# A hybrid decoder layer: thirteen of the MLP's 22 column-tile pairs by Strassen's scheme

## The chip, the cores and the metric

The kernel runs on one core of one Trainium2 chip. The metric is the device time of one execution in microseconds (us). The core has five engines with a queue each: TensorE (PE; its weight loads are a row of their own, PEld), VectorE (DVE), ScalarE (ACT), GpSimd (POOL) and SyncE (SP), which here only issues transfers.

## The reference

One decoder layer on 512 tokens of width 1024, all in float32. Three token mixers (a gated short convolution, block-sparse attention, cross-attention to a memory) are gated, merged and projected, and a residual is added. The change touches what follows:

```
h2 = rmsnorm(x, g_ffn)
a, b = jnp.split(h2 @ w_up, 2, axis=-1)        # w_up: 1024 x 5632
a = causal_dwconv3(a, ffn_conv_w, ffn_conv_b)   # three taps over positions, per channel
x = x + (jax.nn.silu(a) * b) @ w_down           # w_down: 2816 x 1024
```

## The kernel before, in words

Activations lie with channels on the 128 partitions and the 512 tokens along the row. A float32 product is made of three matmuls on a rounded format, `mm3`: each operand is split into a high part (rounded, by ScalarE) and a low part (the rest, by VectorE), and high x high, low x high and high x low add up in one PSUM bank (L235 to L237). A block of weights is 128x128; `weight_units` lists the blocks in the order of use, and they lie in that order in memory. They come in pieces of eight blocks (512 KB, three `raw` buffers, `load_piece`, issued by SP at L180). `cut_steps` makes the high part of a piece on ScalarE (`hi`, L197) and the low part on VectorE (`lo`, L200), with three buffers of each.

w_up has 44 column tiles of 128: 22 for `a`, 22 for `b`; tile f of `a` and tile f of `b` make a pair. The first two pairs run side by side (`proj_outer`: for each of eight row blocks k, four banks). Each later pair is two tiles of eight blocks, so 48 matmuls of 512 columns (`proj_inner`). The inputs `h2` are x times the gain, not yet divided by the norm. That factor, `r2b`, one number per token spread over the partitions, is multiplied in when a bank is read (L871, L878). `ffn_a` reads the bank of `a` into `u`, whose first two columns GpSimd clears, runs the three taps (`conv3`: one ScalarE and two VectorE instructions, L582 to L584) and SiLU (L873); `ffn_b` reads the bank of `b`, multiplies (L879) and splits the product for w_down (L242, L244). w_down then takes four column tiles at once, three singly and the last in two halves of 256 tokens.

The order of TensorE's instructions is that of the program. On the other four engines a scheduler sets the order of each queue when the program is built; each engine then runs its queue strictly in that order, each instruction waiting for what it needs.

Of the kernel before, what the change touches and what calls it, by code (L numbers as in the profile page):

```python
# [59 lines left out]
def weight_units():  # L60

    u = []

    def inner(m, c, nk):
        u.extend((m, k, c) for k in range(nk))

    def outer(m, cs, nk):
        u.extend((m, k, c) for k in range(nk) for c in cs)

    outer("w_in", range(T_QM, T_QM + 4), KD)  # L70
    for c in range(4):
        inner("w_mem_kv", c, KD)
    outer("w_mem_kv", range(4, 8), KD)
    for c in range(4):
        for t in (T_C, T_X, T_B):
            inner("w_in", t + c, KD)
    for p in range(4):
        if p == 3:
            outer("w_in", range(T_V, T_V + 4), KD)
        inner("w_in", T_Q + p, KD)  # L80
        inner("w_in", T_K + p, KD)
    for g, m, ahead in ((0, "w_br_conv", 0), (2, "w_br_mem", 0), (1, "w_br_moba", AHEAD)):
        n = max(ahead, 1)
# [27 lines left out]
def layer_kernel(ctx: ExitStack, tc: tile.TileContext, xT, memT, vecs, ws, outT):  # L111
    nc = tc.nc
    units = weight_units()
    sizes = piece_sizes(len(units))

    cp = ctx.enter_context(tc.tile_pool(name="cp", bufs=1))
    wp = ctx.enter_context(tc.tile_pool(name="wp", bufs=3))
    tp = ctx.enter_context(tc.tile_pool(name="tp", bufs=10))
    ps = ctx.enter_context(tc.tile_pool(name="ps", bufs=1, space=bass.MemoryType.PSUM))
    hp = ctx.enter_context(tc.tile_pool(name="hp", bufs=16))  # L120
    mp = ctx.enter_context(tc.tile_pool(name="mp", bufs=8))
# [13 lines left out]
    def bank(tag="acc"):  # L135
        return ps.tile([P, 512], F32, tag=tag, name=nm(tag), bufs=PSB[tag])
# [232 lines left out]
    start = ExitStack()  # L369
# [47 lines left out]
    mh, hx, qm_n, kk, km, vm = ([] for _ in range(6))  # L417
# [65 lines left out]
    first = []  # L483
# [354 lines left out]
    x2, h2 = [], []  # L838
    ss_2 = yp.tile([P, S], F32, tag="yr", name="ss_2", bufs=7)

    def residual(acc, k):
# [3 lines left out]
        split(hl, x, V("g_ffn", k))  # L845
        x2.append(x)
# [12 lines left out]
    mid.close()  # L859


    fp = ctx.enter_context(tc.tile_pool(name="fp", bufs=2 * NF))
    r2b = fp.tile([P, S], F32, tag="r2b", name="r2b", bufs=1)
    mlp = []
    for _ in row_steps(r2b, small(16), ss_2):
        pass

    def ffn_a(acc, f):
        u = tp.tile([P, S + 2], F32, tag="u", name=nm("u"), bufs=2)
        nc.gpsimd.memset(u[:, 0:2], 0.0)  # L870
        nc.vector.tensor_mul(u[:, 2 : S + 2], acc, r2b)  # L871
        t = conv3(u, [V("f_w", NF * i + f) for i in range(3)], V("f_b", f))
        nc.scalar.activation(t, t, AF.Silu)  # L873
        return t

    def ffn_b(acc, t):
        b = tmp()
        nc.vector.tensor_mul(b, acc, r2b)  # L878
        nc.vector.tensor_mul(b, b, t)  # L879
        hl = tuple(fp.tile([P, S], FR, tag="m", name=nm("m")) for _ in range(2))  # L880
        split(hl, b)
# [82 lines left out]
```

## Time and profile before

| | |
|---|---|
| median of 3 runs | 843.8 us (841.82 to 844.9) |
| the profiled execution | 844.19 us |
| its span, first to last instruction | 842.4 us |
| TensorE busy | 834.2 us, 3714 matmuls |
| VectorE / ScalarE / GpSimd busy | 519.9 / 380.8 / 46.2 us |
| w_up, from its first to its last matmul's start | 469.1 to 715.3 us |
| w_down | 715.5 us to the end |
| mean granted TensorE clock | 0.997 of 2.4 GHz |

Matmuls overlap in the trace: one of 512 columns is shown as 0.39 us long, but the next starts before it ends. What a row of them costs is read from the distance between starts. VectorE's instructions overlap a little too, so for them as well the distance between starts is the price in a full queue, and the duration is the time until somebody else can use the result.

### The profile page before, as it was taken

To read this page: it belongs to the slowest core of one execution; us is meant where nothing else is said; L and a number is where in the kernel's file an instruction comes from. 1 tells how busy PE (TensorE), PEld (TensorE's weight loads), DVE (VectorE), ACT (ScalarE), POOL (GpSimd) and SP (SyncE) were. 2 spreads that over 40 slices of the span, in tenths; PEclk is the share of its full clock that TensorE was granted. 3 is DMA by queue.
4 is the path that set the end of the run, shared out by engine and by line. 5 is a ranking of instruction groups with operands and counts; after the bars stand their busy time and mean duration, and the time that the engine had idled before them with its cause. 6 is when DMAs were issued, how large, how long until landed. Compare 5 with 4: busy or idle time off the path is not lost.

```text
span 842.4 us, 9986 instructions
## 1 busy us (share of the span) xinstructions
PE 834.2 (99%) x3714; PEld 679.3 (81%) x3714; DVE 519.9 (62%) x834; ACT 380.8 (45%) x682; POOL 46.2 (5%) x97
## 2 busy tenths in 40 slices
PE   8999999999999999999999999999999999999998
PEld 6788888888888888888888888888888888888888
DVE  5998898957767776755547575565556655323221
ACT  6666776637645655553324453333333333222110
POOL 0200000101221101110000000000000000000000
PEclk9999999999999999999999999999999999999999
DMA  8353222433333332225223223322332232223410
GB/s 298 112 172 101 96 76 80 123 114 105 100 100 113 95 100 75 82 93 177 99 100 100 79 96 100 100 83 92 100 101 85 90 100 100 96 81 128 135 63 26
DMA packets 26594, 87.76 MB, mean 104 GB/s; under 512 B 3121, under 2 KB 3761, under 8 KB 26417
## 3 DMA queue, kind: packets, MB, share of 16 engines
q1 hardware_dynamic: 26400, 87.04, 31.9%
q8 instruction: 29, 0.48, 0.2%
q14 instruction: 21, 0.16, 0.1%
q10 hardware_dynamic: 144, 0.08, 0.0%
HBM read 81.87 MB, written 2.10 MB: 100 GB/s over the span
## 4 chain that ended last, share of the span: by engine, by line
PE 95%; DMA 2%; DVE 2%; issue 0%; ACT 0%; SPq 0%; DVEq 0%; ACTq 0%
PE acc L237 25%; PE acc L236 25%; PE acc L235 25%; PE s L236 6%; PE s L237 6%; PE s L235 6%; PE m L752 1%; DMA raw<-ws 1%; PE s L693 1%; DMA xr<-xT 1%; PE s L694 1%; DVE lo L200 0%; DVE mh L248 0%; DVE ss_x L433 0%; PE m L237 0%
## 5 line engine op out<-in xcount | busy, mean ns | idle before, releaser
L197 ACT ACTIVATE hi<-raw 128x1024 fp32r<-128x1024 f32 (+1 forms) x148 | 154.9, 1047 | 263.8 <-PE acc L237 154.9
L200 DVE TENSOR_TENSOR lo<-raw,hi 128x1024 fp32r<-128x1024 f32 (+1 forms) x148 | 179.4, 1213 | 152.5 <-ACT hi L197 152.2
L237 PE MATMUL acc<-h,hi 128*128 128x512 f32 x568 | 224.3, 395 | 0.0
L235 PE MATMUL acc<-h,hi 128*128 128x512 f32 x568 | 224.3, 395 | 0.0
L236 PE MATMUL acc<-h,lo 128*128 128x512 f32 x568 | 224.2, 395 | 0.0
L237 PEld LDWEIGHTS acc<-h,hi 128*128 128x128 f32 x568 | 106.8, 188 | 25.5
L236 PEld LDWEIGHTS acc<-h,lo 128*128 128x128 f32 x568 | 106.8, 188 | 24.9
L235 PEld LDWEIGHTS acc<-h,hi 128*128 128x128 f32 x568 | 106.8, 188 | 24.7
L236 PE MATMUL acc<-m,lo 128*128 128x512 f32 (+1 forms) x132 | 47.1, 357 | 0.0
L235 PE MATMUL acc<-m,hi 128*128 128x512 f32 (+1 forms) x132 | 47.1, 357 | 0.0
L237 PE MATMUL acc<-m,hi 128*128 128x512 f32 (+1 forms) x132 | 47.1, 357 | 0.0
L235 PE MATMUL s<-h,hi 128*128 128x512 f32 x112 | 44.2, 395 | 0.0
L236 PE MATMUL s<-h,lo 128*128 128x512 f32 x112 | 44.2, 395 | 0.0
L237 PE MATMUL s<-h,hi 128*128 128x512 f32 x112 | 44.2, 395 | 0.0
L300 ACT ACTIVATE ty<-ty 32x16 f32<-32x16 f32 (+4 forms) x136 | 29.1, 214 | 16.4 <-DVE ty L281 8.0
L873 ACT ACTIVATE tmp<-tmp 128x512 f32<-128x512 f32 x22 | 14.0, 636 | 41.2 <-DVE tmp L584 41.1
L871 DVE TENSOR_TENSOR u<-acc,r2b 128x512 f32<-128x512 f32 x15 | 10.4, 692 | 31.7 <-PE acc L237 31.7
L236 PEld LDWEIGHTS acc<-m,lo 128*128 128x128 f32 x132 | 24.8, 188 | 4.1
L235 PEld LDWEIGHTS acc<-m,hi 128*128 128x128 f32 x132 | 24.8, 188 | 4.0
L237 PEld LDWEIGHTS acc<-m,hi 128*128 128x128 f32 x132 | 24.8, 188 | 4.0
L780 ACT ACTIVATE tmp<-acc,half_b 128x512 f32<-128x512 f32 x21 | 14.5, 688 | 29.9 <-PE acc L237 29.8
L235 PE MATMUL s<-m,hi 128*128 128x512 f32 x66 | 26.1, 395 | 0.0
(218 smaller groups left out, 1359.7 us busy)
## 6 DMA issues: line engine op xcount, KB each, us to landing
raw<-ws SPq DMA_DIRECT2D x145, 512.0 KB, 3.3
xr<-xT SPq DMA_DIRECT2D x8, 256.0 KB, 5.7
xres<-xT SPq DMA_DIRECT2D x1, 2048.0 KB, 9.5
outT<-tmp SPq DMA_DIRECT2D x7, 256.0 KB, 3.1
qh<-qh SPq DMA_DIRECT2D x12, 128.0 KB, 2.3
ql<-ql SPq DMA_DIRECT2D x12, 128.0 KB, 2.3
mr<-memT SPq DMA_DIRECT2D x4, 256.0 KB, 7.7
raw<-ws SPq DMA_DIRECT2D x2, 128.0 KB, 3.1
```

Source lines behind the costliest of these rows:

```text
L197: nc.scalar.activation(hi[:, :m], raw[:, :m], AF.Copy)
L200: nc.vector.tensor_sub(lo[:, :m], raw[:, :m], hi[:, :m].bitcast(F32))
L235: nc.tensor.matmul(out, l[0], r[0], start=start, stop=False)
L236: nc.tensor.matmul(out, l[1], r[0], start=False, stop=False)
L237: nc.tensor.matmul(out, l[0], r[1], start=False, stop=stop)
L300: nc.scalar.activation(dst, src, AF.Copy)
L693: nc.tensor.matmul(acc[:, :n], l, q_hi[:, q0:], start=True, stop=False)
L694: nc.tensor.matmul(acc[:, :n], l, q_lo[:, q0:], start=False, stop=True)
L752: nc.tensor.matmul(acc[:, i0:], l, b[:, : S - i0], start=i == 0 and b is x[0], stop=i == 3 and b is x[1],)
L780: nc.scalar.activation(z, acc, AF.Tanh, bias=half_b[:, i : i + 1], scale=0.5)
L871: nc.vector.tensor_mul(u[:, 2 : S + 2], acc, r2b)
L873: nc.scalar.activation(t, t, AF.Silu)
```

## The change

For 13 pairs (FAST: f = 3 to 5, 7 to 9, 11 to 13, 15 to 17 and 19) the product of a pair is done by Strassen's scheme, in the form with 15 additions. The matrix of weights for a pair is cut in four: rows 0 to 511 and 512 to 1023 (four blocks k each), columns of `a` and of `b`. The inputs are cut in four in the same way: channels, and tokens 0 to 255 and 256 to 511. Seven products of a quarter with a quarter take the place of eight. Each is four blocks k of three matmuls with 256 columns (`product`), so a pair has 84 matmuls of 256 columns in place of 48 of 512.

What is added around them:

- The factor `r2b` is now multiplied into x after the first two pairs (`hn`: eight VectorE multiplies and eight splits), and the other pairs read no `r2b`.
- Four sums of the inputs (`sums`, from 16 VectorE subtractions of 256 columns and eight splits) are made once.
- For each fast pair, `cut_fast` makes four sums of the weights: three by VectorE (s3, s2, s4, into `sx`), the fourth, a21 + a22, by a transfer that GpSimd issues and that adds to its destination in place. Then it splits all seven operands.
- For the 18 pieces of w_up that are not in fast pairs the low part is no longer a VectorE subtraction: ScalarE writes the negated high part, and a GpSimd transfer adds the raw weights to it.
- Seven reads of PSUM per fast pair add the products up (`fast_tiles`: two by ScalarE, five by VectorE, 256 columns each), four banks x, y, z, w, of which three take a second product.
- Products for w_down are kept whole (`mf`) and split after the last pair. x itself goes to memory and is read back for the last residual.

```diff
+FAST = frozenset((3, 4, 5, 7, 8, 9, 11, 12, 13, 15, 16, 17, 19))
...
         nc.scalar.activation(hi[:, :m], raw[:, :m], AF.Copy)
         st["cut"] = i + 1
         yield
-        nc.vector.tensor_sub(lo[:, :m], raw[:, :m], hi[:, :m].bitcast(F32))
+        if units[sum(sizes[:i])][0] == "w_up":
+
+            nc.scalar.activation(lo[:, :m], raw[:, :m], AF.Copy, scale=-1.0)
+            nc.gpsimd.dma_start(lo[:, :m], raw[:, :m], accum_op=ALU.add)
+        else:
+            nc.vector.tensor_sub(lo[:, :m], raw[:, :m], hi[:, :m].bitcast(F32))
...
+    hn = []
+    for k in range(KD):
+        nc.vector.scalar_tensor_tensor(
+            x2[k], x2[k], V("g_ffn", k), r2b, op0=ALU.mult, op1=ALU.mult
+        )
+        hl = tuple(hp.tile([P, S], FR, tag="h", name=nm("hn")) for _ in range(2))
+        split(hl, x2[k])
+        hn.append(hl)
+
+    sums = [[] for _ in range(4)]
+    for k in range(0, KH, 2):
+        raw = [tmp() for _ in range(4)]
+        for i in range(2):
+            top, low, c = x2[k + i], x2[k + i + KH], slice(H * i, H * i + H)
+            t1, t2, t3, t4 = (r[:, c] for r in raw)
+            nc.vector.tensor_sub(t1, top[:, H:], top[:, :H])
+            nc.vector.tensor_sub(t2, low[:, H:], t1)
+            nc.vector.tensor_sub(t3, low[:, H:], top[:, H:])
+            nc.vector.tensor_sub(t4, low[:, :H], t2)
+        for n, r in enumerate(raw):
+            hl = tuple(fs.tile([P, S], FR, tag="t", name=nm("t"), bufs=16) for _ in range(2))
+            split(hl, r)
+            sums[n].extend(tuple(a[:, H * i : H * i + H] for a in hl) for i in range(2))
...
+    def cut_fast():
...
+        nc.vector.tensor_sub(s3, a11, a21)
+        nc.vector.tensor_sub(s2, a22, s3)
+        nc.vector.tensor_sub(s4, a12, s2)
+        nc.gpsimd.dma_start(a21, a22, accum_op=ALU.add)
+        f1 = tuple(wp.tile([P, 2 * n], FR, tag=t, name=nm(t), bufs=3) for t in ("hi", "lo"))
+        fx = tuple(fs.tile([P, 3 * n], FR, tag=t, name=nm(t), bufs=2) for t in ("hx", "lx"))
+        f2 = tuple(wp.tile([P, 2 * n], FR, tag=t, name=nm(t), bufs=3) for t in ("hi", "lo"))
+        split(tuple(a[:, :n] for a in f1), a11)
+        split(fx, sx)
+        split(tuple(a[:, n:] for a in f1), a21)
+        split(f2, r2)
...
+    def product(out, l, r, first):
+        for k in range(KH):
+            w = tuple(a[:, k * P : (k + 1) * P] for a in l)
+            for x, (a, b) in enumerate(((w[0], r[k][0]), (w[1], r[k][0]), (w[0], r[k][1]))):
+                nc.tensor.matmul(
+                    out[:, :H], a, b, start=first and k == 0 and x == 0,
+                    stop=k == KH - 1 and x == 2, skip_group_check=not first,
+                )
+
+    def fast_tiles(f, l, tags):
...
+        product(x, a11, rows(0, 0), True)
+        nc.scalar.activation(v1, x[:, :H], AF.Copy)
+        product(y, s2, sums[1], True)
+        nc.vector.tensor_add(v2, y[:, :H], v1)
+        product(z, s3, sums[2], True)
+        nc.vector.tensor_add(v1, z[:, :H], v2)
+        product(w, s1, sums[0], True)
+        nc.vector.tensor_add(b[:, H:], w[:, :H], v1)
+        product(x, a12, rows(KH, 0), False)
+        nc.scalar.activation(u[:, 2 : H + 2], x[:, :H], AF.Copy)
+        product(z, a22, sums[3], False)
+        nc.vector.tensor_add(b[:, :H], z[:, :H], v2)
+        product(w, s4, rows(KH, H), False)
+        nc.vector.tensor_add(u[:, H + 2 :], w[:, :H], v2)
+        gated(conv3(u, *taps(f)), b)
...
     for f in range(2, NF):
-        tag = "s" if f % 3 == 2 else "acc"
-        t = ffn_a(proj_inner("w_up", f, h2, tag=tag), f)
-        ffn_b(proj_inner("w_up", NF + f, h2, tag=tag), t)
...
+        tags = ("acc",) * 4 if f % 2 == 0 else ("s", "m", "s", "m")
+        if f in FAST:
+            fast_tiles(f, left, tags)
```

The scheduler's order changes with it, at three places that the prediction speaks of. On VectorE, where the first two pairs end, the queue before holds the bank reads of pairs 0 and 1, their taps, and the low parts of the next weights (`u`, `tmp`: the two pairs; `lo`: weights; the number in a name tells tiles apart):

```order
L871 TENSOR_TENSOR u_929_4646<-acc_913_4522,r2b_4501 128x512
L878 TENSOR_TENSOR tmp_931_4654<-acc_914_4523,r2b_4501 128x512
L871 TENSOR_TENSOR u_934_4661<-acc_915_4524,r2b_4501 128x512
L583 SCALAR_TENSOR_TENSOR tmp_930_4649<-u_929_4646,vec_77,tmp_930_4649 128x512
L878 TENSOR_TENSOR tmp_936_4669<-acc_916_4525,r2b_4501 128x512
L584 SCALAR_TENSOR_TENSOR tmp_930_4649<-u_929_4646,vec_77,tmp_930_4649 128x512
L200 TENSOR_TENSOR lo_941_4678<-raw_925_4590,hi_940_4677 128x1024
```

Now 42 instructions stand from the read of the first bank (`u_929`) up to `t_972`, the low part of the second half of `sums[1]`. These are the last of them (`t_...`: split sums of the inputs; `lo_1001`, `sx_999`: weights of pair 4; `tmp_978`: taps of pair 2):

```order
L257 TENSOR_TENSOR t_964_4755<-tmp_956_4733,t_963_4754 128x512
L257 TENSOR_TENSOR t_970_4771<-tmp_965_4758,t_969_4770 128x512
L952 TENSOR_TENSOR sx_999_4972<-raw_998_4970,sx_999_4972 128x512
L930 TENSOR_TENSOR tmp_968_4761<-x2_896_4457,tmp_966_4759 128x256
L896 TENSOR_TENSOR mf_936_4687<-tmp_935_4685,tmp_934_4681 128x512
L1006 SCALAR_TENSOR_TENSOR tmp_978_4811<-acc_977_4786,vec_77,tmp_978_4811 128x511
L930 TENSOR_TENSOR tmp_968_4761<-x2_904_4499,tmp_966_4759 128x256
L257 TENSOR_TENSOR lo_1001_4978<-raw_997_4968,hi_1000_4977 128x512
L257 TENSOR_TENSOR t_972_4775<-tmp_966_4759,t_971_4774 128x512
```

So the sums of the inputs stand behind the taps of pairs 0 to 2 and between parts of the weights of pairs 3 and 4. On TensorE the second product of pair 3 (bank `m_989`) takes that tile after its first half:

```order
L972 MATMUL m_989_4863<-t_959_4746,hx_984_4850 128x256
L972 MATMUL m_989_4863<-t_959_4746,lx_985_4851 128x256
L972 MATMUL m_989_4863<-t_960_4747,hx_984_4850 128x256
L972 MATMUL m_989_4863<-t_971_4774,hx_984_4850 128x256
L972 MATMUL m_989_4863<-t_971_4774,lx_985_4851 128x256
L972 MATMUL m_989_4863<-t_972_4775,hx_984_4850 128x256
```

On GpSimd the queue before held only the clearings of `u` here:

```order
L870 MEMSET u_943_4707 128x2
L870 MEMSET u_956_4784 128x2
L870 MEMSET u_969_4861 128x2
L870 MEMSET u_982_4938 128x2
L870 MEMSET u_995_5015 128x2
```

Now the adding transfers stand between them (`raw` into `raw`: the sum a21 + a22 of a fast pair; `raw` into `lo`: a low part of a plain pair; here from the clearing for pair 7 to the first piece of pair 10):

```order
L981 MEMSET u_1056_5324 128x2
L954 DMA raw_1040_5241<-raw_1041_5243 128x512
L211 DMA lo_1038_5236<-raw_1036_5233 128x1024
L981 MEMSET u_1074_5453 128x2
L954 DMA raw_1061_5426<-raw_1062_5428 128x512
L954 DMA raw_1079_5555<-raw_1080_5557 128x512
L981 MEMSET u_1092_5582 128x2
L211 DMA lo_1099_5687<-raw_1097_5684 128x1024
```

There are two `u` buffers, so a clearing waits until the taps two fast pairs earlier have been read, and the transfers behind it wait with it.

## Rows read from the trace of the kernel before

**Rows 1.** The page: busy time of each engine, and the chain that ended last.
```profile
PE 834.2 (99%) x3714; PEld 679.3 (81%) x3714; DVE 519.9 (62%) x834; ACT 380.8 (45%) x682; POOL 46.2 (5%) x97
...
PE 95%; DMA 2%; DVE 2%; issue 0%; ACT 0%; SPq 0%; DVEq 0%; ACTq 0%
```
**Rows 2.** Windows: length, then busy PE, PEld, DVE, ACT, POOL, PEclk, DMA, GB/s.
```profile
469.00:491.50 22.50, 22.50 (x99) 18.08 (x98) 12.07 (x23) 9.29 (x11) 0.00 (x0) 1.00 0.30 94
491.50:603.00 111.50, 111.50 (x479) 89.71 (x478) 68.27 (x87) 44.74 (x55) 1.19 (x12) 1.00 0.29 94
```
**Rows 3.** Timeline of PE: start, us, instruction; where w_up starts and later.
```profile
469.07 0.40 PE L235 MATMUL acc<-h,hi 128*128 128x512 f32 x1
...
491.47 0.40 PE L235 MATMUL s<-h,hi 128*128 128x512 f32 x1
...
494.27 0.40 PE L235 MATMUL s<-h,hi 128*128 128x512 f32 x1
```
**Rows 4.** Timeline of PE and of PEld, last column tile, 256 columns.
```profile
828.02 0.28 PE L236 MATMUL acc<-m,lo 128*128 128x256 f32 x1
...
834.08 0.28 PE L236 MATMUL acc<-m,lo 128*128 128x256 f32 x1
...
823.28 0.19 PEld L236 LDWEIGHTS acc<-m,lo 128*128 128x128 f32 x1
823.40 0.19 PEld L237 LDWEIGHTS acc<-m,hi 128*128 128x128 f32 x1
```
**Rows 5.** Windows early in the run, and PE's timeline inside them.
```profile
33.00:35.00 2.00, 1.51 (x8) 1.00 (x8) 2.00 (x3) 0.00 (x0) 1.84 (x3) 1.00 0.00 0
35.00:37.00 2.00, 0.83 (x5) 0.72 (x4) 2.00 (x2) 1.06 (x1) 0.15 (x1) 0.74 0.00 0
37.00:39.00 2.00, 2.00 (x11) 2.00 (x10) 2.00 (x4) 0.00 (x0) 0.00 (x0) 0.50 0.91 274
...
37.09 0.41 PE L236 MATMUL s<-mh,lo 128*128 128x256 f32 x1
37.30 0.41 PE L237 MATMUL s<-mh,hi 128*128 128x256 f32 x1
```
**Rows 6.** Timeline of DVE: four instructions of a full queue, then r2b.
```profile
449.31 1.22 DVE L200 TENSOR_TENSOR lo<-raw,hi 128x1024 fp32r<-128x1024 f32 x1
450.44 0.69 DVE L853 TENSOR_TENSOR ss<-ss,tmp 128x512 f32<-128x512 f32 x1
451.05 0.75 DVE L248 SCALAR_TENSOR_TENSOR h<-x,vec,h 128x512 fp32r<-128x512 f32 x1
451.71 0.68 DVE L853 TENSOR_TENSOR ss<-ss,tmp 128x512 f32<-128x512 f32 x1
...
479.80 0.71 DVE L288 STREAM_TRANSPOSE r2b<-ty 128x512 f32<-128x512 f32 x1
```
**Rows 7.** Timeline of DVE: the first read of a w_up bank.
```profile
489.58 0.69 DVE L871 TENSOR_TENSOR u<-acc,r2b 128x512 f32<-128x512 f32 x1 [1.18 <-PE acc L237]
```
**Rows 8.** Groups of ACT in w_up: busy, mean ns, idle before.
```profile
L197 ACT ACTIVATE hi<-raw 128x1024 fp32r<-128x1024 f32 x44 | 46.7, 1062 | 100.2 <-PE acc L237 65.4 <-PE s L237 27.9 <-issue 6.8
...
L242 ACT ACTIVATE m<-tmp 128x512 fp32r<-128x512 f32 x21 | 13.3, 633 | 9.0 <-DVE tmp L879 8.9
```
**Rows 9.** The page: transfers, KB each, median us from issue to landing.
```profile
raw<-ws SPq DMA_DIRECT2D x145, 512.0 KB, 3.3
...
xres<-xT SPq DMA_DIRECT2D x1, 2048.0 KB, 9.5
outT<-tmp SPq DMA_DIRECT2D x7, 256.0 KB, 3.1
qh<-qh SPq DMA_DIRECT2D x12, 128.0 KB, 2.3
```
**Rows 10.** POOL: a clearing of u in the timeline, and its longest group.
```profile
493.71 0.10 POOL L870 MEMSET u<- 128x2 f32 x1 [126.44 <-DVE tmp L584]
...
L711 POOL PARTITION_ALL_REDUCE mb<-tmp x8 | 14.7, 1843 | 10.9 <-DVE tmp L709 10.9
```

More of the change, by code (lines that the diff above doesn't have):

```diff
@@ L94, in weight_units @@
     for f in range(2, NF):
-        inner("w_up", f, KD)
-        inner("w_up", NF + f, KD)
+        if f in FAST:
+            for ks in (range(4), range(4, KD)):
+                for c in (f, NF + f):
+                    u.extend(("w_up", k, c) for k in ks)
+        else:
+            inner("w_up", f, KD)
+            inner("w_up", NF + f, KD)
     outer("w_down", range(4), NF)
@@ L839, in layer_kernel @@
     ss_2 = yp.tile([P, S], F32, tag="yr", name="ss_2", bufs=7)
+    dp = ctx.enter_context(tc.tile_pool(name="dp", bufs=1, space=bass.MemoryType.DRAM))
+    x2d = dp.tile([KD, P, S], F32, name="x2d")
     def residual(acc, k):
@@ L845, in residual @@
         split(hl, x, V("g_ffn", k))
+        nc.sync.dma_start(x2d[k], x)
         x2.append(x)
@@ L859, in layer_kernel @@
     mid.close()
-    fp = ctx.enter_context(tc.tile_pool(name="fp", bufs=2 * NF))
-    r2b = fp.tile([P, S], F32, tag="r2b", name="r2b", bufs=1)
-    mlp = []
+    H = S // 2
+    KH = KD // 2
+    fm = ctx.enter_context(tc.tile_pool(name="fm", bufs=NF - 8, reuse_waits="tile"))
+    fast = ExitStack()
+    fs = fast.enter_context(tc.tile_pool(name="fs", bufs=1, reuse_waits="tile"))
+    r2b = fm.tile([P, S], F32, tag="r2b", name="r2b", bufs=1)
+    mf = []
     for _ in row_steps(r2b, small(16), ss_2):
@@ L866, in layer_kernel, with taps, gated @@
         pass
-    def ffn_a(acc, f):
+    def taps(f):
+        return [V("f_w", NF * i + f) for i in range(3)], V("f_b", f)
+    def gated(t, b):
+        pool, tag = (fm, "mf") if len(mf) < NF - 8 else (mp, "mj")
+        m = pool.tile([P, S], F32, tag=tag, name=nm("mf"))
+        nc.scalar.activation(t, t, AF.Silu)
+        nc.vector.tensor_mul(m, b, t)
+        mf.append(m)
+    accs = proj_outer("w_up", (0, NF, 1, NF + 1), h2, ["acc"] * 4)
+    st["look"] = 0
+    for f in range(2):
         u = tp.tile([P, S + 2], F32, tag="u", name=nm("u"), bufs=2)
@@ L870, in ffn_a @@
         nc.gpsimd.memset(u[:, 0:2], 0.0)
[L871 to L876, printed above, removed]
-        b = tmp()
[L878 to L881, printed above, removed]
-        mlp.append(hl)
-    accs = proj_outer("w_up", (0, NF, 1, NF + 1), h2, ["acc"] * 4)
@@ L885, in layer_kernel @@
-    for f in range(2):
-        ffn_b(accs[2 * f + 1], ffn_a(accs[2 * f], f))
-    for f in range(2, NF):
-        tag = "s" if f % 3 == 2 else "acc"
-        t = ffn_a(proj_inner("w_up", f, h2, tag=tag), f)
-        ffn_b(proj_inner("w_up", NF + f, h2, tag=tag), t)
-    def finish(acc, c, cols=slice(0, S)):
-        o = tmp()
-        nc.vector.tensor_add(o[:, cols], acc[:, cols], x2[c][:, cols])
+        nc.vector.tensor_mul(u[:, 2 : S + 2], accs[2 * f], r2b)
+        t = conv3(u, *taps(f))
+        b = tmp()
@@ new lines, in layer_kernel @@
+        nc.vector.tensor_mul(b, accs[2 * f + 1], r2b)
+        gated(t, b)
+    hn = []
[20 more added lines that the diff above has]
+            sums[n].extend(tuple(a[:, H * i : H * i + H] for a in hl) for i in range(2))
@@ new lines, in rows, with part @@
+    def rows(k0, c0):
+        return [tuple(a[:, c0 : c0 + H] for a in hn[k]) for k in range(k0, k0 + KH)]
+    def cut_fast():
+        i = st["cut"]
+        while st["loaded"] < i + 2:
+            load_piece()
+        r1, r2 = raws.pop(i), raws.pop(i + 1)
+        st["cut"] = i + 2
+        n = KH * P
+        a11, a21 = r1[:, :n], r1[:, n:]
+        a12, a22 = r2[:, :n], r2[:, n:]
+        sx = fs.tile([P, 3 * n], F32, tag="sx", name=nm("sx"))
+        s2, s3, s4 = (sx[:, n * j : n * j + n] for j in range(3))
+        nc.vector.tensor_sub(s3, a11, a21)
[9 more added lines that the diff above has]
+        split(f2, r2)
+        def part(hl, j):
+            return tuple(a[:, n * j : n * j + n] for a in hl)
+        return part(f1, 0), part(fx, 0), part(fx, 1), part(f1, 1), part(f2, 0), part(f2, 1), part(fx, 2)
@@ new lines, in product @@
+    def product(out, l, r, first):
[7 more added lines that the diff above has]
+    def fast_tiles(f, l, tags):
+        a11, s2, s3, s1, a12, a22, s4 = l
+        x, y, z, w = (bank(t) for t in tags)
+        u = tp.tile([P, S + 2], F32, tag="u", name=nm("u"), bufs=2)
+        nc.gpsimd.memset(u[:, 0:2], 0.0)
+        b, v = tmp(), tmp()
+        v1, v2 = v[:, :H], v[:, H:]
+        product(x, a11, rows(0, 0), True)
[13 more added lines that the diff above has]
+        gated(conv3(u, *taps(f)), b)
@@ new lines, in plain_tiles, with cut_next @@
+    def plain_tiles(f, tags):
+        acc = proj_inner("w_up", f, hn, tag=tags[0])
+        ws, bias = taps(f)
+        t = tmp()
+        nc.scalar.activation(t, acc, AF.Identity, bias=bias, scale=ws[2])
+        for i in (1, 2):
+            nc.vector.scalar_tensor_tensor(
+                t[:, i:], acc[:, : S - i], ws[2 - i], t[:, i:], op0=ALU.mult, op1=ALU.add
+            )
+        gated(t, proj_inner("w_up", NF + f, hn, tag=tags[1]))
+    def cut_next(f):
+        if f in FAST:
+            return cut_fast()
+        for _ in range(2 if f < NF else 0):
+            while st["cut"] < st["use"] + 2:
+                cut_piece()
@@ new lines, in layer_kernel @@
+    left = None
+    for f in range(2, NF):
+        tags = ("acc",) * 4 if f % 2 == 0 else ("s", "m", "s", "m")
+        if f in FAST:
+            fast_tiles(f, left, tags)
+            st["u"] += 2 * KD
+            st["use"] += 2
+        else:
+            plain_tiles(f, tags)
+        if f == max(FAST):
+            fast.close()
+        left = cut_next(f + 1)
+    st["look"] = LOOK
+    fd = ctx.enter_context(tc.tile_pool(name="fd", bufs=2 * NF - 16, reuse_waits="tile"))
+    mlp = []
+    for f in range(NF):
+        pool, tag = (fd, "m") if f < NF - 8 else (hp, "h")
+        hl = tuple(pool.tile([P, S], FR, tag=tag, name=nm("m")) for _ in range(2))
+        split(hl, mf[f])
+        mlp.append(hl)
@@ L895, in finish, with stream @@
+    def stream(c):
+        x = tmp()
+        nc.sync.dma_start(x, x2d[c])
+        return x
+    def finish(acc, c, o, cols=slice(0, S)):
+        nc.vector.tensor_add(o[:, cols], acc[:, cols], o[:, cols])
         nc.sync.dma_start(outT[c * P : (c + 1) * P, cols], o[:, cols])
+    outs = [stream(c) for c in range(4)]
     for c, acc in enumerate(proj_outer("w_down", range(4), mlp, ["acc"] * 4)):
-        finish(acc, c)
+        finish(acc, c, outs[c])
     for c in range(4, 7):
-        finish(proj_inner("w_down", c, mlp, tag="s"), c)
+        o = stream(c)
+        finish(proj_inner("w_down", c, mlp, tag="s"), c, o)
@@ L902, in layer_kernel @@
     parts = [(bank(), slice(0, S // 2)), (bank(), slice(S // 2, S))]
     head = NF - 8
+    o = stream(7)
     ws = []
@@ L912, in layer_kernel @@
             mm3(acc[:, cols], ws[k], tuple(a[:, cols] for a in mlp[k]), False, k == NF - 1)
-        finish(acc, 7, cols)
+        finish(acc, 7, o, cols)
 def kernel(**inputs):
```

1 line of the change is left out of this document (added).

## The prediction, written before the result was known

> **What bounds the kernel now.** I read the page's busy times and its chain first: TensorE is busy 99% of the span and the chain runs through it for 95% [rows 1]. Then I cut w_up out by windows: in 491.5 to 603 us TensorE is busy 111.5 of 111.5 us at a granted clock of 1.00, VectorE 68.3, ScalarE 44.7 [rows 2]. Last, TensorE's own timeline: twelve matmuls of 512 columns start in 494.27 - 491.47 = 2.80 us, 0.2333 us each, and two pairs (96 matmuls) take 491.47 - 469.07 = 22.40 us, again 0.2333 [rows 3]. So here TensorE waits for nothing. Every matmul's worth that goes is time won, as long as nobody makes TensorE wait; every wait that comes in is time lost, since no gap can swallow it. The sum is therefore: work removed from TensorE, against waits put in.
>
> **What goes.** A pair now is 48 x 0.2333 = 11.20 us. A fast pair is 84 matmuls of 256 columns. Such matmuls stand in the last column tile: 51 steps in 834.08 - 828.02 = 6.06 us, 0.119 us each [rows 4], hence 84 x 0.119 = 10.00 us. 1.20 us per pair, 13 pairs: **15.6 us less**. An eighth of the columns goes, but a short matmul costs 2% more than half a long one.
>
> A rule of the Trainium skill speaks against this term ("TensorE: Matmul & The Clock Gate", Part 3, what overlaps and what doesn't): a weight load overlaps matmuls in flight only when it goes to another group of the array's rows. Rows 4 show loads over all 128 rows, 0.19 us long and 0.12 us apart, beside steps of 0.119 us: the rule does not hold for this kernel.
>
> **What it puts on the other engines.** By steps in a full queue VectorE's instruction costs 1.13 us at 1024 columns, 0.61 at 512, 0.66 for one with a scalar and two tensors [rows 6]; a line through the first two gives 0.35 at 256 and 1.65 at 1536 (estimates). A fast pair asks three weight sums (1.83), the low parts (2 x 0.61 + 1.65 + 1.13 = 4.00), five reads of banks (1.75), two taps (1.32) and a gate product (0.61): 9.5 us in TensorE's 10.0. A plain pair keeps 1.9 us, since its low parts leave VectorE. Averaged over w_up it fits; inside a fast pair nothing may be late. ScalarE's per-pair sum (its 1024-column copy is 1.06 us, its 512-column one 0.63 [rows 8]) stays under 7 us.
>
> **Front, a wait on VectorE (certain to come; its size is the main term).** r2b's write ends at 480.5 [rows 6]; I put it at 481.0, as one more ScalarE copy stands ahead. From then the queue has 8 multiplies by r2b (8 x 0.66 = 5.3) and 9 subtractions (5.5) ahead of the first bank read, which so starts near 491.8 and not at 489.58 [rows 7]; TensorE's pair 2 starts about 1.1 us late. From that read to t_972, 42 instructions: 19 of 512 columns (11.6), 16 of 256 (5.6), 5 taps (3.3), one each of 1024 and 1536 (2.8) = 23.3 us, so t_972 starts at 515.1 and is there at 515.8. TensorE wants it after pair 2 (491.47 + 11.20), pair 3's first product (1.43) and half of the second (0.71), with 0.24 of starts between: 505.05. **10.7 us lost.** Within it, t_971 comes from ScalarE, where it stands behind hi_1000, which waits for an adding transfer; it does not come later than VectorE's own queue allows. Behind the wait nothing is late at once: the scheduler's next weights go on being cut.
>
> **Clock.** TensorE would stand about 5 us and then 3 us with six matmuls between. The trace shows one such place: after a stretch of 8 and then 5 matmuls in 2 us each, the granted clock is 0.74 and then 0.50 (the 1.2 GHz level), and 256-column starts are 0.214 us apart instead of 0.119 [rows 5]. It ran low for 3.4 us there. The same here costs 3.4 x (1 - 0.119/0.214) = **1.5 us**. Bounds 0 and 3.
>
> **Adding transfers.** 18 of 512 KB (low parts of plain pieces) and 13 of 256 KB (a21 + a22) are issued by GpSimd and read what they write. The trace has none. Nearest rows from below: a raw load of 512 KB, 3.3 us, and a copy of 128 KB, 2.3 [rows 9]. From above a second read is added: 2 MB takes 9.5 us and 512 KB 3.3, 4.13 us per MB, so 512 KB more is 2.1 us: 5.4; and 256 KB, 3.1 + 1.0 = 4.1. I take the middle of each, 4.4 and 3.2 us, and 1 us of GpSimd per issue (0.10 for a clearing, 1.84 for its longest instruction [rows 10]). What follows a fast pair's transfer is fixed: raw buffer free, next load (3.3), transfer, ScalarE's copies, VectorE's low part, 9.5 us plus the transfer, against 12.4 us of TensorE's work from that buffer's release to its use in the next pair. So with 3.2 it is 0.3 us over in the second and third pair of a run of three. On GpSimd the transfers stand behind the clearings of u, so one late tap keeps back the weights of a later pair. On ScalarE and VectorE a copy that waits for a transfer holds the next bank's read behind it.
>
> I laid the five queues of w_up end to end in their new order with the durations above. Waits of TensorE from 469 us on, all told (front included):
>
> - transfers 3.3 and 2.3 us: 11.2 us
> - 4.4 and 3.2: 12.6 us (GpSimd at 0.5 or 1.5 us an issue: 11.9, 14.1)
> - 5.0 and 3.6: 18.0 us
> - 5.4 and 3.7: 21.3 us
> - 6.0 and 4.8: 30.4 us
>
> Up to 4.4 only the front counts; beyond it each fast pair pays about 1.3 us twice, as the first read of its last banks waits.
>
> **Costed at nothing.** The added factor and the sums beyond the front, and the reads of r2b that go, are VectorE's, not on the path later. Storing x and reading it back adds SP issues that nobody waits for before the last residual. w_down's first weights are loaded under w_up's last pairs; the 22 late splits (ScalarE 22 x 0.63 = 13.9 us, VectorE about 13.4) run beside pairs 20 and 21 and w_down's first tiles, 14 row blocks of 12 matmuls, 39 us of TensorE's work, before the last ones are wanted. If that cover is gone they cost up to 13 us, less the idle time of VectorE there; I see no place for more than 1.
>
> **Sum**, against the profiled execution of 844.19 us (842.4 of span, 1.8 around it): 844.2 - 15.6 + 12.6 + 1.5 = 842.7. It lies 0.4 above the median of 843.8, so the forecast is **842.3 us**: gain and waits nearly cancel. No change that a measurement of this kernel can tell, within 0.5%, is 839.6 to 848.0.
>
> **Rivals.**
>
> 1. *Slower: the adding transfers set the pace.* Mechanism: in a fast pair VectorE reads two tensors in nearly every instruction, and GpSimd cannot get its transfers out between them. If each waits for the end of a VectorE instruction, at most 1.65 us, 4.4 and 3.2 become 6.0 and 4.8, waits are 30.4, and the time 844.2 - 15.6 + 30.4 + 1.5 - 0.4 = 860.1 us. Merely the upper end of the transfers (5.4 and 3.7) gives 851.0. It decides from 18.3 us of waits, that is from about 5.0 us per 512 KB. For it: VectorE 9.5 of 10.0 us in a fast pair, no such transfer in the trace, a sum that grows steeply past 4.4. Against: 18 + 13 transfers in some 235 us leave the DMA engines, at 0.29 of their time now [rows 2], far from full. The Trainium skill ("SBUF — State Buffer", Who interferes with whom) says that a VectorE instruction with two inputs in SBUF gets in the way of a GpSimd instruction that reads SBUF, while it infers that preparing a transfer, which writes, is spared; the two readings are this rival and the forecast, and no row of before shows either. Chance 0.33.
> 2. *Faster: the waits are smaller than laid out.* If the transfers take no longer than the raw loads (11.2 us) and the clock stays up, 844.2 - 15.6 + 11.2 - 0.4 = 839.4 us. If the 42 instructions also overlap more (20 us in place of 23.3), 836.1. For it: VectorE's instructions overlap already [rows 6], and a short one may cost less than my 0.35. Against: the front stands in one strict queue, and its other rows are measured. Centre 837.7, chance 0.28.
> 3. *The change does not do what it says*: a short matmul waits for its weights. With load and matmul in turn (0.19 + 0.107 = 0.295 us, half a long step for the matmul) a pair takes 24.8 us and the run some 1020. Rows 4 exclude it for a run of 51; chance 0.01.
>
> **How the numbers follow.** Forecast 0.38, with a range of its own of 839.6 to 848.0; rival 1 0.33, rival 2 0.28, rival 3 0.01. So faster by over 0.5% 0.28, within it 0.38, slower 0.34. The range of 8 in 10 reaches from 836 (rival 2's low end) to 859, just under rival 1's full price, with the rest of rivals 1 and 3 outside.
>
> **What would show it.** Products at 0.119 us a step and 10.0 us a fast pair: the gain. One wait of some 8 us near 505 to 516, ended by VectorE's or ScalarE's t tiles, and a start of pair 2 about 1 us late: the front; without it, rival 2. A granted clock of 0.50 for 3 to 4 us behind it. Landing times of GpSimd's transfers in the list of issues: 4.4 and 3.2, under 3.5 for rival 2, over 5 for rival 1, which also shows waits of 1.3 us at the last banks of each fast pair. w_up should end near 712 and w_down keep its length. Wrong at the root would be a step of 256 columns over 0.13 us, or a wait of more than 2 us in w_down.

## The result: slower by 1.0%

The changed kernel takes 852.07 us (median of 4 runs, 850.5 to 854.19) against 844.15 for the kernel before (4 runs, 841.82 to 844.9): a ratio of 1.010, 95% interval 1.007 to 1.013. The forecast of no measurable change, 842.3 us, was wrong; the time lies near the lower price of the first rival, 851.0 us, which put the adding transfers at the upper end of their bounds. That it lies so near is in part luck, as the account below shows.

The page of the profiled execution (852.0 us, span 850.0): busy times, the chain that ended last, and the transfers, to be held against [rows 1] and [rows 9].

```profile
PE 825.4 (97%) x4182; PEld 697.6 (82%) x4182; DVE 559.7 (66%) x946; ACT 430.9 (51%) x768; POOL 75.4 (9%) x121
...
PE 78%; DMA 11%; DVE 6%; issue 3%; ACT 1%; POOL 0%; SPq 0%; POOLq 0%; DVEq 0%
...
raw<-ws SPq DMA_DIRECT2D x145, 512.0 KB, 3.2
lo<-raw POOLq DMA_DIRECT2D x18, 512.0 KB, 5.5
raw<-raw POOLq DMA_DIRECT2D x13, 256.0 KB, 3.3
```

The chain is no longer nearly all TensorE: 11% of it are transfers and 6% VectorE. The adding transfers of 512 KB land after 5.5 us (4.5 to 8.0), those of 256 KB after 3.3 (3.2 to 3.6).

What TensorE waits for in w_up (waits of the changed kernel from 469 to 730 us: total, times, longest):

```profile
PE acc L248 <- DVE u L905: 5.6, 1, 5.6
PE m L972 <- ACT t L255: 3.9, 1, 3.9
PE s L972 <- DVE tmp L989: 3.6, 3, 1.2
PE acc L972 <- DVE tmp L989: 3.3, 3, 1.1
PE m L972 <- DVE t L257: 2.0, 1, 2.0
PE s L972 <- ACT tmp L985: 0.6, 2, 0.4
PE acc L249 <- DMA lo<-raw: 0.2, 1, 0.2
```

Two places: the front (5.6 before pair 2; 3.9 and 2.0 inside pair 3's second product), and six waits of 1.1 to 1.2 us at the bank that VectorE reads in L989 (the third product), two in each later run of three fast pairs. The front on TensorE's timeline (start, length, instruction, idle before it and what ended it):

```profile
493.22 0.77 PE L248 MATMUL acc<-hn,hi 128*128 128x512 f32 x1 [5.63 <-DVE u L905]
...
513.21 0.58 PE L972 MATMUL m<-t,hx 128*128 128x256 f32 x1 [3.88 <-ACT t L255]
513.59 0.42 PE L972 MATMUL m<-t,lx 128*128 128x256 f32 x1
516.03 0.80 PE L972 MATMUL m<-t,hx 128*128 128x256 f32 x2 [2.02 <-DVE t L257]
516.62 0.41 PE L972 MATMUL m<-t,lx 128*128 128x256 f32 x1
```

and what VectorE does ahead of the first of these waits:

```profile
484.14 0.69 DVE L951 TENSOR_TENSOR sx<-raw 128x512 f32<-128x512 f32 x1 [1.00 <-DMA raw<-ws]
484.75 3.09 DVE L257 TENSOR_TENSOR hn<-x,hn 128x512 fp32r<-128x512 f32 x5
491.18 0.69 DVE L952 TENSOR_TENSOR sx<-raw,sx 128x512 f32<-128x512 f32 x1 [3.34 <-DMA raw<-ws]
491.79 0.68 DVE L257 TENSOR_TENSOR hn<-x,hn 128x512 fp32r<-128x512 f32 x1
492.39 0.68 DVE L905 TENSOR_TENSOR u<-acc,r2b 128x512 f32<-128x512 f32 x1
```

VectorE stands twice, 4.34 us in all, at a sum of pair 3's weights, with the read of TensorE's first bank (u, L905) queued behind it. The pieces are late because SP, which issues their loads, waits for buffers that adding transfers hold (waits of SP's queue, 465 to 480 us):

```profile
SPq L188 <- DMA lo<-raw: 17.7, 3, 7.6
```

The same picture in the first later run of three: VectorE at the sums of the next pair's weights, then TensorE at the bank that VectorE reads too late.

```profile
553.63 0.69 DVE L951 TENSOR_TENSOR sx<-raw 128x512 f32<-128x512 f32 x1 [3.02 <-DMA raw<-ws]
554.24 0.74 DVE L597 SCALAR_TENSOR_TENSOR tmp<-u,vec,tmp 128x512 f32<-128x512 f32 x1
556.24 0.69 DVE L952 TENSOR_TENSOR sx<-raw,sx 128x512 f32<-128x512 f32 x1 [1.25 <-DMA raw<-ws]
```

```profile
565.57 0.39 PE L972 MATMUL s<-t,hi 128*128 128x256 f32 x1 [1.21 <-DVE tmp L989]
```

The second wait of that run has ScalarE in its chain as well: it stands for the 256 KB transfer before it can copy a21 + a22, and VectorE's next low parts come behind that copy.

```profile
571.37 0.63 ACT L255 ACTIVATE hi<-raw 128x512 fp32r<-128x512 f32 x1 [3.40 <-DMA raw<-raw]
...
577.21 0.39 PE L972 MATMUL acc<-t,hi 128*128 128x256 f32 x1 [1.13 <-DVE tmp L989]
```

**The account.** By the starts on TensorE's timeline w_up takes 258.1 us instead of 246.4, 11.7 more; w_down, from its first to its last matmul's start, takes 123.1 instead of 123.35. These are the starts of w_up, of the first pair behind the front, and of w_down in the changed kernel:

```profile
465.02 0.40 PE L248 MATMUL acc<-h,hi 128*128 128x512 f32 x1
...
545.22 0.39 PE L248 MATMUL acc<-hn,hi 128*128 128x512 f32 x1
...
723.16 0.41 PE L248 MATMUL acc<-m,hi 128*128 128x512 f32 x1
```

Against pairs of 11.15 (plain) and 10.01 us (fast) without a wait, the front (the first two pairs, pair 2 and the first run of three) takes 80.2 instead of 63.6, **16.6 lost**; the later runs of three take 33.8, 33.1 and 33.6 instead of 30.0, **10.5 lost**; 0.4 is lost at one plain pair. 27.5 lost, 15.6 gained.

The profiled executions differ by only 7.8 us, because that of before began w_up at 469.07 [rows 3] and this one at 465.02. These 4 us arise in the first 41 us. There TensorE stands 1.17 us in the kernel before and then runs at the low clock for a dozen matmuls [rows 5], and the changed kernel does neither; the same matmul, the 161st, starts at 40.50 in the first and at 36.40 in the second (the last line), and from there to w_up the two stay 4.1 us apart:

```profile
36.29 0.58 PE L236 MATMUL s<-mh,lo 128*128 128x256 f32 x1 [1.17 <-DVE lo L200]
...
40.50 0.28 PE L235 MATMUL acc<-mh,hi 128*128 128x256 f32 x1
...
36.40 0.28 PE L248 MATMUL acc<-mh,hi 128*128 128x256 f32 x1
```

So far ahead the five queues hold the same instructions in the same order; they differ from 441 us on, with the stores of x. Another execution of the kernel before (841.62 us) began w_up at 466.49:

```profile
466.49 0.40 PE L235 MATMUL acc<-h,hi 128*128 128x512 f32 x1
```

So I don't count these 4 us as an effect of the new scheme. But they are not one execution's chance either: the medians differ by 7.9 us too, and of the 11 profiles with the change (this one and the kernels below, 464.8 to 468.3) nine began w_up by 466.0. Why the kernels with the change mostly start early is left open. It follows that a ratio a little under 1 can be the early start alone, and that an edit's effect is better read from the length of w_up, which stands below beside each time (before 246.4, changed 258.1).

### The profile page after: what moved, and what is told of

Same layout as the page of the kernel before. It is cut to its first block, busy times and chain, and to the rows that moved or that the text cites. A ratio compares the mean times of both kernels' runs of the same rounds, so it can differ in the third digit from the quotient of the medians.

```text
span 850.0 us, 11243 instructions
## 1 busy us (share of the span) xinstructions
PE 825.4 (97%) x4182; PEld 697.6 (82%) x4182; DVE 559.7 (66%) x946; ACT 430.9 (51%) x768; POOL 75.4 (9%) x121
## 3 DMA queue, kind: packets, MB, share of 16 engines
q1 hardware_dynamic: 28704, 91.24, 32.0%
q0 software_dynamic: 4464, 12.85, 8.4%
## 4 chain that ended last, share of the span: by engine, by line
PE 78%; DMA 11%; DVE 6%; issue 3%; ACT 1%; POOL 0%; SPq 0%; POOLq 0%; DVEq 0%
PE acc L249 20%; PE acc L248 20%; PE acc L250 20%; DMA raw<-ws 5%; DMA lo<-raw 5%; PE s L249 3%; PE s L248 3%; PE s L250 3%; PE s L972 2%; PE acc L972 2%; PE m L972 1%; DMA raw<-raw 1%; DVE lo L257 1%; PE m L765 1%; DVE lx L257 1%
## 5 line engine op out<-in xcount | busy, mean ns | idle before, releaser
L213 DVE TENSOR_TENSOR lo<-raw,hi 128x1024 fp32r<-128x1024 f32 (+2 forms) x104 | 125.3, 1206 | 133.4 <-ACT hi L205 133.1
L205 ACT ACTIVATE hi<-raw 128x1024 fp32r<-128x1024 f32 (+2 forms) x122 | 126.9, 1041 | 149.7 <-PE acc L250 90.0
L250 PE MATMUL acc<-h,hi 128*128 128x512 f32 x360 | 142.3, 395 | 0.0
L248 PE MATMUL acc<-h,hi 128*128 128x512 f32 x360 | 142.2, 395 | 0.0
L249 PE MATMUL acc<-h,lo 128*128 128x512 f32 x360 | 142.2, 395 | 0.0
L250 PEld LDWEIGHTS acc<-h,hi 128*128 128x128 f32 x360 | 67.7, 188 | 16.1
L249 PEld LDWEIGHTS acc<-h,lo 128*128 128x128 f32 x360 | 67.8, 188 | 15.3
L248 PEld LDWEIGHTS acc<-h,hi 128*128 128x128 f32 x360 | 67.8, 188 | 15.2
L255 ACT ACTIVATE hi<-raw 128x512 fp32r<-128x512 f32 (+1 forms) x39 | 29.6, 767 | 31.2 <-DMA raw<-raw 14.6
L248 PE MATMUL acc<-hn,hi 128*128 128x512 f32 x96 | 39.2, 408 | 5.6 <-DVE u L905 5.6
L249 PE MATMUL acc<-hn,lo 128*128 128x512 f32 x96 | 39.0, 406 | 0.2 <-DMA lo<-raw 0.2
L250 PE MATMUL acc<-hn,hi 128*128 128x512 f32 x96 | 38.9, 405 | 0.0
L313 ACT ACTIVATE ty<-ty 32x16 f32<-32x16 f32 (+4 forms) x136 | 29.1, 214 | 16.4 <-DVE ty L294 8.0
L257 DVE TENSOR_TENSOR lo<-raw,hi 128x512 fp32r<-128x512 f32 (+1 forms) x39 | 33.0, 862 | 5.9 <-ACT hi L255 5.9
```

The source lines that it names most:

```text
L248: nc.tensor.matmul(out, l[0], r[0], start=start, stop=False)
L249: nc.tensor.matmul(out, l[1], r[0], start=False, stop=False)
L250: nc.tensor.matmul(out, l[0], r[1], start=False, stop=stop)
L255: nc.scalar.activation(hi, src, AF.Copy)
L257: nc.vector.tensor_sub(lo, src, hi.bitcast(F32))
L313: nc.scalar.activation(dst, src, AF.Copy)
```

## The experiments

Two theories stood against each other. A: the 512 KB transfers hold raw buffers, pieces come late, VectorE's queue stands at a weight sum. B: VectorE simply has too much to do. Two more came up on the way: C, that the 256 KB transfers delay the runs of three, and D, that the transfers' own length decides and not the buffers that they hold. Each time below stands beside the kernel before on the same chip.

**Low parts by VectorE (lo_vector).**

```diff
-        if units[sum(sizes[:i])][0] == "w_up":
-            nc.scalar.activation(lo[:, :m], raw[:, :m], AF.Copy, scale=-1.0)
-            nc.gpsimd.dma_start(lo[:, :m], raw[:, :m], accum_op=ALU.add)
-        else:
-            nc.vector.tensor_sub(lo[:, :m], raw[:, :m], hi[:, :m].bitcast(F32))
+        nc.vector.tensor_sub(lo[:, :m], raw[:, :m], hi[:, :m].bitcast(F32))
```

> The low parts of the 18 plain pieces of w_up are VectorE subtractions again; everything else is as in the changed kernel. Theory A (the 512 KB adding transfers take 5.5 us and more, hold a raw buffer that long, the next piece of weights comes late, and VectorE's queue stands at a weight sum with a bank's read behind it): the six waits of 1.1 to 1.2 us at second products go to 0, the wait before pair 2 falls from 5.6 to about 2 us, the waits at pair 3's sums of the inputs stay or grow to 6 to 10 us; time 840 to 844 us against 852 of the changed kernel. Theory B (VectorE has too much work in the front and in runs of three fast pairs, the transfers only relieve it): the six waits stay, the front grows by some 4.5 us for four more subtractions of 1.13 us, 852 to 858 us.

841.23 us, ratio 0.9977 (0.9963 to 0.9991), w_up 247.3: 10.8 less than the changed kernel, and still 0.9 more in w_up than before, so the ratio under 1 is the early start. TensorE's waits in w_up, and the start and end of the first later run of three (f = 7 to 9):

```profile
PE m L972 <- DVE t L257: 7.3, 2, 4.4
PE m L972 <- ACT t L255: 3.4, 2, 3.2
PE acc L248 <- DVE u L905: 2.1, 1, 2.1
```

```profile
555.93 0.28 PE L972 MATMUL s<-hn,hi 128*128 128x256 f32 x1
...
585.96 0.39 PE L248 MATMUL acc<-hn,hi 128*128 128x512 f32 x1
```

A holds for the runs of three: 30.03 us, 252 matmuls at 0.119. For the front it does not: the wait before pair 2 falls to 2.1 as expected, but the two behind it grow to 10.7, and the front loses 16.3 us, as much as with transfers.

**The sum a21 + a22 by VectorE (sum_vector).** `nc.gpsimd.dma_start(a21, a22, accum_op=ALU.add)` becomes `nc.vector.tensor_add(a21, a21, a22)`.

> The sums a21 + a22 of the 13 fast pairs are VectorE additions; the low parts of the plain pieces stay with the transfers. Theory A: the wait before pair 2 and the front stay within 1 us, the waits in the runs of three shrink to about a third (three of 0.5 us), 847 to 850 us. Theory C (the 256 KB transfers, for which ScalarE waited 14.6 us in nine places, are what delays the runs of three): these waits are gone and nothing else changes, 845 to 847. Theory B: 13 more instructions of 0.61 us inside fast pairs, waits there grow, over 853 us.

845.13 us, ratio 1.0024 (1.0009 to 1.0039), w_up 251.9. One wait of 1.4 us is left in the runs of three (30.0, 30.1, 31.7 us), as C has it, though the first experiment cleared these runs with the 256 KB transfers in place. A and C had expected the front to stay as it was, and it did not: it takes 83.2 us instead of 80.2, with waits of 6.3, 4.2 and 2.9, as the additions now stand in VectorE's queue there (this reason was not tested by itself). So the time lies in C's range by two differences that cancel in part: the runs of three and the plain pairs gain 9.2, the front loses 3.0. Either kind of transfer alone is bearable in the runs of three; the two together on three buffers are not.

**No transfers (no_transfers).** Both edits together.

> Neither kind of adding transfer: low parts and the sums a21 + a22 by VectorE. Theory A: like the kernel with VectorE's low parts, within 1.5 us of it, 841 to 845 us, no wait in the runs of three. Theory B: the slowest of the four, 855 us or more.

840.54 us, ratio 0.9974 (0.9957 to 0.999), w_up 247.4: a little under the range of A, and in w_up 0.9 more than before. B falls for the runs of three, which take 30.0 us each. In the front, the windows from 479 to 517 us of the changed kernel and of this one (length, busy PE, PEld, DVE, ACT, POOL, clock, DMA, GB/s) say why nothing is gained:

```profile
479.00:517.00 38.00, 26.47 (x109) 21.26 (x108) 33.66 (x60) 21.54 (x33) 3.62 (x6) 0.85 0.46 114
```

```profile
479.00:517.00 38.00, 27.02 (x115) 21.67 (x114) 38.00 (x65) 20.39 (x30) 0.20 (x2) 0.83 0.21 69
```

The 4.34 us in which VectorE stood are now filled, with two low parts of 1.22 us and two of the additions of 0.68 among others; it is busy 38.00 of 38.00. The front loses 16.7 us, as much as with both transfers.

**Pairs 3 to 5 plain (late_fast).** `FAST` without 3, 4, 5; transfers stay.

> Pairs 3 to 5 are plain, ten fast pairs stay (7 to 9, 11 to 13, 15 to 17, 19), transfers as in the changed kernel. Both theories: the front's waits (5.6, 3.9 and 2.0 us, and the stretch at the low clock behind them) go, since the sums of the inputs are not wanted before pair 7. Theory A: four or so waits of 1.1 to 1.2 us are left in two runs of three; 844.2 - 10 x 1.20 + 5 = 837 to 839 us, faster than before. Theory B: the extra work of VectorE is only moved, a wait of several us stays around pairs 6 and 7, 843 to 848 us.

840.86 us, ratio 0.9969 (0.995 to 0.9987), about 2 over the range of A. By w_up the miss is larger: 245.5 us, 0.9 less than before where A's sum has 7 less. The front's waits are gone; the runs of three keep theirs, and 1.9 us are waited for low parts:

```profile
PE s L972 <- DVE tmp L989: 3.5, 3, 1.3
PE acc L972 <- DVE tmp L989: 2.4, 3, 1.1
PE acc L249 <- DMA lo<-raw: 1.9, 2, 1.1
```

**A fourth raw buffer (raw4).** Transfers as in the changed kernel; one of the ten temporary row buffers goes to make room.

```diff
-        raw = wp.tile([P, 8 * P], F32, tag="raw", name=nm("raw"), bufs=3)
+        pool, tag, bufs = (fs, "rawx", 1) if st["x"] and i % 4 == 3 else (wp, "raw", 3)
+        raw = pool.tile([P, 8 * P], F32, tag=tag, name=nm("raw"), bufs=bufs)
```

> The changed kernel with both kinds of transfers, but every fourth piece of w_up from pair 2 to pair 16 goes into a fourth raw buffer (one temporary row buffer fewer, to make room). Theory A (a transfer holds a raw buffer, the next piece is late, VectorE stands at a weight sum): the six waits at second products go to under 2 us in all, and VectorE's two waits for pieces in the front (1.0 and 3.3 us) shrink; 840 to 845 us. Rival D (not the buffer but the transfers' own length decides, since ScalarE's copy of a21 + a22 and TensorE wait for what they deliver): the waits stay, 850 to 853 us.

842.29 us, ratio 0.998 (0.9967 to 0.9992), w_up 248.7. With the same transfers the six waits are gone: the buffer they hold is the cause in the runs of three, and D falls there. (Their length is nearly the same: 4.9 us at the median for 512 KB instead of 5.5, and 3.5 for 256 KB instead of 3.3.) In the front the expectation missed: VectorE still waits 5.1 us for pieces, TensorE 6.5, 3.4 and 2.7, and the front takes 81.5 us.

**Without the sums of the inputs (no_sums).** No transfers, and `sums` is replaced by quarters of `hn`; the four sums of the inputs are left out.

> The kernel without transfers, 13 fast pairs from pair 3 on, but the four sums of the inputs are left out: the products take quarters of the inputs themselves in their place. Theory B for the front (VectorE's queue, not the transfers, sets when pair 3's second product can go on): 16 x 0.35 + 8 x 0.61 = 10.5 us less on VectorE ahead of it, the 9 us of waits inside pair 3 fall to 1 or less and the low clock goes with them; 840.5 - 10.5 to 12 = 828 to 830 us. If the loads of the weights or the splits of the inputs set the front, 836 us or more.

828.15 us, ratio 0.9812 (0.9791 to 0.9834), w_up 235.4, 12.4 less than no_transfers (12.0 in w_up). All that TensorE still waits for in w_up:

```profile
PE acc L248 <- DVE u L905: 2.1, 1, 2.1
PE acc L973 <- DVE tmp L992: 0.4, 1, 0.4
```

So it is the sums that TensorE waits for behind pair 2, and not the loads of the weights or the splits of the inputs. This run takes out more than VectorE's 10.5 us, though: ScalarE's eight copies go as well, and TensorE no longer waits for sums at all. That VectorE's queue is what makes the sums late is read from no_transfers, where it is busy 38.00 of 38.00 us.

**One fast pair (one_fast).** `FAST = frozenset((19,))`, so 42 pieces of w_up go by transfer.

> Only pair 19 is fast, all other pieces of w_up get their low part by an adding transfer, 42 of them. Theory A (the transfers cost only where VectorE's queue stands at a weight sum behind them): no wait of note, 843.5 - 1.2 = 842 us, at most 844. Rival D (the transfers cost by themselves, 5.5 us in the chain of each plain piece): waits of TensorE for low parts in most pairs, 850 us or more.

840.71 us, ratio 0.9959 (0.9944 to 0.9974), below A's 842 and more than one pair can give. In its profile w_up takes 245.3, 1.1 less than before, about what one pair gives; the rest would be an early start in most of its runs, of which there is no profile. TensorE waits nowhere in w_up. The window from 500 to 640 us and the transfers:

```profile
500.00:640.00 140.00, 140.00 (x602) 112.63 (x601) 35.26 (x54) 70.08 (x82) 21.49 (x25) 1.00 0.83 188
...
lo<-raw POOLq DMA_DIRECT2D x42, 512.0 KB, 5.9
```

Transfers of 5.9 us in the chain of every piece cost nothing in plain pairs, where VectorE is 25% busy and no weight sum stands in its queue.

**Fillers (filler).** On no_transfers, matmuls that nobody reads, where TensorE waits in pair 3.

```diff
-        product(y, s2, sums[1], True)
+        product(y, s2, sums[1], True, (w, (0, 18, 30, 22)) if f == 3 else None)
```

> The kernel without transfers and with fast pairs from 3 on, with 70 matmuls of 256 columns more that nobody reads, on operands that are already there, in the three places of pair 3's second product where TensorE waits for the sums of the inputs (18, 30 and 22: 2.1, 3.6 and 2.6 us). VectorE's queue is the same, so the last of these sums comes at the same time. If TensorE's low clock behind the waits is a cost of its own: granted clock 1.00 from 511 on, starts 0.119 instead of 0.214 us apart in the 28 or so matmuls behind, 2.6 us less, 837.5 to 838.5 us against 840.5. If the fillers only displace work or the clock is no cost: 840.5 or more.

841.52 us, ratio 0.9979 (0.9963 to 0.9995), w_up 247.3 as in no_transfers: no gain. The first of the three waits came ahead of the place where I had put 18 fillers, so these ran where nothing was waited for, and the rest ran late. But the clock answers. First no_transfers, then fillers; windows that hold the matmuls behind the last wait:

```profile
514.80:520.70 5.90, 5.87 (x27) 5.87 (x28) 5.90 (x10) 0.63 (x1) 0.00 (x0) 0.50 0.17 67
```

```profile
515.00:522.00 7.00, 6.99 (x59) 6.79 (x58) 7.00 (x11) 1.00 (x2) 0.00 (x0) 1.00 0.23 75
```

From the last waiting matmul to the fourth product's first, the same work takes 520.95 - 514.83 = 6.12 us at 0.50 and 521.99 - 518.77 = 3.22 at 1.00. The low clock cost 2.9 us there, and the badly placed fillers as much.

**Fast pairs 5 to 19 (fast_5_to_19).** No transfers, `FAST = frozenset(range(5, 20))`.

> No transfers, and the fast pairs are 5 to 19 without a gap, 15 of them. By the queues laid end to end with the durations of the trace: waits 1.4 before pair 2, 0.8 at pair 5 and four of 0.2, 3.1 in all; 843.5 - 15 x 1.20 + 3.1 = 828.6 us, 827 to 832, faster than both kernels. If VectorE with 10.1 us of work per fast pair cannot keep up over 15 in a row: a wait in every pair, 835 to 845.

825.88 us, ratio 0.9785 (0.9765 to 0.9805): faster than both kernels, and 1.1 under the range expected. w_up takes 231.5 us, 14.9 less than before, which is the sum expected (15 x 1.20 - 3.1 = 14.9); the rest of the time gained is the early start. TensorE waits for 1.5 and 0.5 us in w_up.

**The same with the 256 KB transfers (fast_5_to_19_pool).**

> Fast pairs 5 to 19, low parts by VectorE, but the sums a21 + a22 again by the 256 KB transfers. If such a transfer costs nothing where no 512 KB transfer shares its queue and its raw buffers: 15 x 0.61 us of VectorE's work go, the waits at pair 5 and behind (1.7 us) go, 823 to 825 us against 825.9. If each transfer still delays the weights: waits at second products, 828 or more.

824.05 us, ratio 0.9763 (0.9741 to 0.9784), w_up 230.0, the best of all and within the range expected. The window over its fast pairs, and its transfers:

```profile
523.00:672.00 149.00, 149.00 (x1253) 149.00 (x1253) 139.44 (x217) 81.92 (x117) 13.30 (x27) 1.00 0.47 129
...
raw<-raw POOLq DMA_DIRECT2D x15, 256.0 KB, 3.3
```

**The kernel before once more (before_again)**, its line shown in the account:

> The kernel before, one more execution with a profile. In the profile of before w_up began at 469.1 us, in that of the changed kernel at 465.0, though the queues hold the same instructions in the same order up to there. If that is a difference between executions, w_up begins somewhere from 464.8 to 469; if the kernel before always begins late, at 468.5 or later.

It began at 466.5, between the two, and its w_up takes 246.40 us again. So executions of one kernel differ by at least 2.6 us ahead of w_up. That the kernels with the change mostly start earlier still is not explained by it.

## Why the prediction was wrong, by its steps

- **The gain, 15.6 us: right.** A run of three fast pairs without waits takes 30.03 us. The Trainium skill's rule on weight loads ("TensorE: Matmul & The Clock Gate", Part 3, what overlaps and what doesn't) again does not hold: in this kernel 252 loads over all rows go on beside matmuls that start 0.119 us apart.
- **The adding transfers: the step that failed.** "I take the middle of each, 4.4 and 3.2 us": the 256 KB one took 3.3, but the 512 KB one 5.5, above the upper bound of 5.4. In the list of the prediction the waits grow from 12.6 to 21.3 us between 4.4 and 5.4 (with 3.2 and 3.7 for the shorter kind), so these durations were worth up to 9 us. The trace has 19.2 us of waits in w_up, 7.7 of them outside the front, where the forecast had next to none: 6.9 in the six waits and 0.8 in three small ones. Raw4 shows the path, the buffer that the transfer holds, by taking it away. "Beyond it each fast pair pays about 1.3 us twice" put the place right and the count too high: two per run of three.
- **The front: count right, standing missed.** VectorE's 42 instructions cost what was said, but the queue was taken to run without a stop. It stood 4.34 us at the weight sums L951 and L952. TensorE went on in pair 3 at 516.03; with w_up's start at 465.02 it should have at 465.02 + 22.40 + 11.20 + 1.43 + 0.71 + 0.24 = 501.0. That is 15.0 late, the forecast's 10.7 and these 4.3. The wait before pair 2, forecast at 1.1, was 5.6 by the same standing.
- **The clock, 1.5 us: right, for one stretch.** From 516.03 the next 15 matmuls take 3.35 us instead of 1.79, 1.6 lost. A second low stretch, behind the 5.6 us before pair 2 (granted clock 0.50 from 495 to 497 us), made pair 2 take 13.8 instead of 11.2 us, but by VectorE's queue TensorE would have waited those 2.6 us in pair 3 anyway (argued, not tried).
- **Costed at nothing: right.** w_down waits for nothing new.
- **Rival 1: its low price came, its mechanism fell.** GpSimd's transfers were not held up by VectorE. They were longest, 5.9 us, where VectorE was busy 25% and the DMA engines 83% (one_fast), and took 3.3 us for 256 KB with VectorE busy 139 of 149 us (fast_5_to_19_pool). The inference of the Trainium skill ("SBUF — State Buffer", Who interferes with whom) that preparing a transfer is spared by VectorE's two-input instructions agrees with both. They took longer beside other transfers: 4.5 to 4.8 us for the last four, 5.5 right behind a 256 KB one, 8.0 in the front, where the loads and stores moved 1.09 MB meanwhile; no run tried this by itself.
- **Rival 3: a slip without effect.** Half a long step is 0.117 us and not 0.107, so load and matmul in turn would be 0.307. The rival did not come: a step was 0.119.

The sum with the measured terms: 844.2 - 15.6 + 16.6 + 10.9 = 856.1, less the 4 us of a different start: 852. Without that start, which nobody forecast, the time would lie 5 us over the 851.0 of the first rival; that it came out so near was luck.

## What to carry to other kernels

Work moved from an engine with room to a transfer does not become free: it holds its source buffer for the transfer's whole length, and in a strict queue the next consumer of that buffer stops all that is behind it. When a sum of waits grows steeply between the bounds of one unmeasured duration, forecast from the steep side or say that the sign is open. And do not start a scheme whose inputs must first be prepared right where the engine that prepares them is fullest: 15 fast pairs that begin two places later, with the low parts back on VectorE, make w_up 16.4 us shorter, where these 13 made it 11.7 longer.

## What the runs showed of the hardware beyond that

- An adding transfer of 512 KB took 5.5 us (median) and 4.5 at best, against 3.2 (median) for a load of the same size; GpSimd was busy 0.86 us with most of them, up to 1.21.
- In the changed kernel's list of queues the transfers from GpSimd move 12.85 MB in 8.4% of the engines' time, those from SP 91.24 MB in 32.0%: nearly twice the time for a byte.

```profile
q1 hardware_dynamic: 28704, 91.24, 32.0%
q0 software_dynamic: 4464, 12.85, 8.4%
```
